# A short causal convolution moved from rows to columns in a two-block decoder on one core

## The chip, the core and the metric

The kernel runs on one core of one Trainium2 chip. It is one launch. The metric is the device time of the whole program in microseconds (us); less is better. The core has five engines with queues of their own: TensorE (PE in the profile, with its weight loads as PEld), VectorE (DVE), ScalarE (ACT), GpSimd (POOL) and SyncE (SP), which here issues all DMAs. Each queue is worked in order.

## What is computed

The program is two layers of a hybrid block and four layers of a second block, on a sequence of 256 rows of 1024 float32 values. The change touches one part of the two hybrid layers, a gated convolution over three neighbouring rows whose 256 columns are the first of the eight column blocks that the mixer's output projection takes:

```python
def short_conv_mixer(gate_b, gate_c, h, conv_w):
    u = gate_c * h
    u_pad = jnp.pad(u, ((0, 0), (CONV_K - 1, 0), (0, 0)))     # CONV_K = 3
    y = conv_w[0] * u_pad[:, 0:S]
    for j in range(1, CONV_K):
        y = y + conv_w[j] * u_pad[:, j:j + S]
    return gate_b * y
```

Row r of the result needs rows r, r-1 and r-2 of u. The result, transposed, is two of the eight 128-row blocks of yT, from which the output projection `mix` is computed; the other six come from two attentions.

## The kernel before

The 256 rows are two tiles of 128, t = 0 and t = 1. Each tile is worked by a generator ("thread") that runs through all layers; a driver at the end of the kernel gives both threads one weight block after another, thread 1 some blocks behind thread 0 (one block in the conv's projections F and H, two in the blocks mkv behind them). A weight block is loaded by one DMA on SP into one of five raw buffers, and split by ACT (the rounded high part, `wh`, L280) and DVE (the rest, `wl`, L233); each product is three matmuls (L322, `mm3`). `proj` (L380) asks for four weight blocks, does six matmuls with each and calls `flush` behind every block. `flush` also works off lists of deferred pieces: `due[t]` holds pairs of a count and a function, and each flush of thread t counts down and calls what has come to 0.

The program is then put in order by a scheduler in the framework, engine by engine, so the order in a queue isn't the order of the code. The tiles come from pools with a fixed number of buffers for each tag; a tile waits until the one that had its buffer has been read for the last time. PSUM banks with the tag `pj` are two for both threads together.

Around the conv, in `mixer` (L608 to L790): the projection F gives gate_b and gate_c, which ACT copies into `cf` (128 x 512, L756). The projection H gives h. DVE multiplies u = gate_c * h (L762). The shifted rows of u are wanted in the partitions of the rows that use them, so two DMAs per tile copy u into `up`, shifted by two rows and by one (L768), and for t = 1 two more bring the last rows of tile 0 (L770). Then DVE multiplies both shifted copies with tap rows `cw` that lie in all partitions (L773), adds (L774), POOL multiplies the third tap (L775), DVE adds it and multiplies with the gate (L776, L777), PE transposes the two halves against the identity (`transpose4`, L275, into `ycp`), and `cut` splits the result into yT's high part (ACT, L313) and low part (DVE, L314).

The projections `mkv` come next (`memory_block`): keys and values of the memory, from `memHi` and `memLo`. Layer 0 has three of these blocks there, layer 1 two. They don't use the conv's result; the output projection `mix` behind them does. The second attention of the layer (`six_heads`: `sp`, `ss`, `ptp`, `ET`) is interleaved with them. All conv instructions run four times: two layers, two tiles.

Of the kernel before, what the change touches and what calls it, by code (L numbers as in the profile page):

```python
# [8 lines left out]
F32 = mybir.dt.float32  # L9
# [3 lines left out]
ALU = mybir.AluOpType  # L13
AX = mybir.AxisListType

P = 128
D = 1024
ALPHA = 4.0 ** 0.25
IALPHA = 1.0 / ALPHA
# [17 lines left out]
EB = ("E", 2)  # L37
# [11 lines left out]
def kernel(  # L49
# [7 lines left out]
    nc = tc.nc  # L57
    V, S, G, T = nc.vector, nc.scalar, nc.gpsimd, nc.tensor

    const = ctx.enter_context(tc.tile_pool(name="const", bufs=1))  # L60
    wr = ctx.enter_context(tc.tile_pool(name="wr", bufs=RBUFS))
    wp = ctx.enter_context(tc.tile_pool(name="wp", bufs=WBUFS))
    sb = ctx.enter_context(tc.tile_pool(name="sb", bufs=1))
# [4 lines left out]
    tiles = {}  # L68
    shared = {}
# [4 lines left out]
    def colblock(key, mat, c0, n, gain=None):  # L74

        v = mat.rearrange("(k p) n -> p k n", p=P)
        for i in range(4):
            plan.append((key + (i,), "w", [P, 2, n], v[:, 2 * i:2 * i + 2, c0:c0 + n],
                         gain and (gain[0], gain[1], 2 * i)))

    def rowblock(key, mat, kts):
        v = mat.rearrange("(k p) n -> p k n", p=P)
        for i, k in enumerate(kts):
            plan.append((key + (i,), "w", [P, 1, D], v[:, k:k + 1, :], None))

    def aux(key, tag, shape, src):
        plan.append((key, tag, shape, src, None))

    def bcast_row(ap2d):
        n = ap2d.shape[-1]  # L90
        return ap2d.broadcast(0, P) if hasattr(ap2d, "broadcast") else ap2d.partition_broadcast(P)

    def memory_blocks(l, pos):
        return [j for j in range(4) if MKV[l, j] == pos]

    def fill(l, which):
        for m in range(2):
            for j in memory_blocks(m, (l, which)):
                colblock(("mkv", m, j), w_mkv[m], 512 * j, 512)
# [4 lines left out]
    for l in range(2):  # L104
        for nm, c0, n in MIXG:
            if nm == "cq" and l == 0:
                for t in range(2):
                    aux(("memr", t), "kv", [P, D], mem[t * P:(t + 1) * P, :])
            if nm == "cq":
                aux(("BT", l), "big8", [P, 6, 256], relx[l])  # L110
                aux(("cw", l), "grow", [P, 3, 256], bcast_row(conv_w[l:l + 1, :, :]))
            colblock((nm, l), w_in[l], c0, n)
        for j in memory_blocks(l, "M"):
            colblock(("mkv", l, j), w_mkv[l], 512 * j, 512)
        rowblock(("mix", l), w_mix[l], MIXK)
        for which in range(3):
            if which == 0:
                fill(l, 0)
            if which == 1:
                for j in range(2):  # L120
                    colblock(("mq", l, j), w_mq[l], 512 * j, 512)
            if l == 1 and which == 2:
                aux(("lnGB",), "big8", [P, 2, D], bcast_row(ln_rows[l, which:which + 1, :, :]))
            if which == 1:
                rowblock(("mo", l), w_mo[l], list(range(8)))
                fill(l, 1)
            if which == 2:
                for j in range(9):
                    if j < 8:
                        colblock(("ff1", l, j), w_ff1[l], 512 * j, 512)  # L130
                    if j > 0:
                        rowblock(("ff2", l, j - 1), w_ff2[l], list(range(4 * j - 4, 4 * j)))
                fill(l, 2)
    FG = [(512 * j, min(512, 2816 - 512 * j)) for j in range(6)]
    for i in range(4):
# [32 lines left out]
        for j in range(7):  # L168
            if j < 6:
                c0, n = FG[j]  # L170
                colblock(("fg", i, j), ffn_in[i], c0, n, (i, 1))
                colblock(("fu", i, j), ffn_in[i], 2816 + c0, n, (i, 1))
            if j > 0:
                c0, n = FG[j - 1]
# [7 lines left out]
    wnum, n = {}, 0  # L182
# [70 lines left out]
    lnc = const.tile([P, 2, 3, 2, 8], F32, name="lnc")  # L253
    ngc = const.tile([P, 4, 3, 8], F32, name="ngc")
    gbs = const.tile([P, 8], F32, name="gbs")

    def load_columns():
        nc.sync.dma_start(lnc, ln_cols)
        nc.sync.dma_start(ngc, ng_cols)
        nc.sync.dma_start(gbs, gm_bs)  # L260

# [10 lines left out]
    def transpose4(t, srcs, nm, kind="tr"):  # L272
        p = bank(kind, t, [P, 4, P], nm)
        for i, s in enumerate(srcs):
            T.transpose(p[:, i, :], s, ident)  # L275
        return p

    def copy(eng, o, i):
        if eng == "s":
            S.copy(o, i)  # L280
        else:
            V.tensor_copy(o, i)
# [23 lines left out]
    def cut(bank, sl, src, scale=1.0, rows=slice(0, P), hi_eng="s"):  # L306

        hi, lo = bank[0][rows, sl, :], bank[1][rows, sl, :]
        if scale == 1.0:
            copy(hi_eng, hi, src)  # L310
            V.tensor_tensor(out=lo, in0=src, in1=hi.bitcast(F32), op=ALU.subtract)
        else:
            S.activation(hi, src, AF.Copy, scale=scale)  # L313
            V.scalar_tensor_tensor(out=lo, in0=src, scalar=scale, in1=hi.bitcast(F32), op0=ALU.mult,  # L314
                                   op1=ALU.subtract)
# [10 lines left out]
    due = ([], [])  # L326
# [260 lines left out]
    def get2(key, shape, tag, bufs=1):  # L587

        if key not in shared:
            shared[key] = sb.tile(shape, F32, tag=tag, name="_".join(str(s) for s in key), bufs=bufs)  # L590
        return shared[key]
# [16 lines left out]
    def mixer(t, l, xT):  # L608
# [4 lines left out]
        yT = Parts()  # L613
# [15 lines left out]
        p = transpose4(t, [I[:, 0:128], I[:, 128:256], ik4.rearrange("p a d -> p (a d)")], "iqp")  # L629
# [10 lines left out]
        p = transpose4(t, [DQ[:, i * P:(i + 1) * P] for i in range(4)], "dqp")  # L640
# [6 lines left out]
        for b0 in (0, 2):  # L647
# [6 lines left out]
            for b in range(2):  # L654
                rv = sb.tile([P, 2, nk], F32, tag=EB[0].format(t=t), name="rl", bufs=EB[1])
                S.activation(rv, ips[b], AF.Relu)
                for i in range(2):
# [3 lines left out]
                    else:  # L661
                        V.scalar_tensor_tensor(out=score, in0=rv[:, i, :], scalar=iws[:, h:h + 1], in1=score,
                                               op0=ALU.mult, op1=ALU.add)
# [91 lines left out]
        cf = sb.tile([P, 512], F32, tag=f"rB{t}", name="cf", bufs=2)  # L755
# [2 lines left out]
                  lambda kt, h: shared[("cv", l, kt)][:, 64 * h:64 * h + 64],  # L758
                  lambda hs: BT[:, hs[0]:hs[-1] + 1:2, 256 - nk:256], lambda j: divmod(2 + j, 4)))
        pH = yield from proj(t, xT, ("H", l), 256)  # L760
        u = get2(("u", l, t), [P, 256], f"U{t}", 3)
        V.tensor_tensor(out=u, in0=cf[:, 256:512], in1=pH[:, 0:256], op=ALU.mult)  # L762

        up = sb.tile([P, 2, 256], F32, tag=EB[0].format(t=t), name="up", bufs=EB[1])
        if t == 0:
            G.memset(up[0:2], 0.0)
        for s_, d in enumerate((2, 1)):
            nc.sync.dma_start(up[d:P, s_, :], u[0:P - d, :])  # L768
            if t == 1:
                nc.sync.dma_start(up[0:d, s_, :], shared[("u", l, 0)][P - d:P, :])  # L770
        cw = tiles[("cw", l)]
        yc = sb.tile([P, 2, 256], F32, tag=f"rB{t}", name="yc", bufs=2)
        V.tensor_tensor(out=yc, in0=up, in1=cw[:, 0:2, :], op=ALU.mult)  # L773
        V.tensor_tensor(out=yc[:, 0, :], in0=yc[:, 0, :], in1=yc[:, 1, :], op=ALU.add)  # L774
        G.tensor_tensor(out=yc[:, 1, :], in0=u, in1=cw[:, 2, :], op=ALU.mult)  # L775
        V.tensor_tensor(out=yc[:, 0, :], in0=yc[:, 0, :], in1=yc[:, 1, :], op=ALU.add)  # L776
        V.tensor_tensor(out=yc[:, 0, :], in0=yc[:, 0, :], in1=cf[:, 0:256], op=ALU.mult)  # L777
        p = transpose4(t, [yc[:, 0, 0:P], yc[:, 0, P:2 * P]], "ycp")
        cut(yT.banks[0], slice(0, 2), p[:, 0:2, :], IALPHA)

        mems = memory_blocks(l, "M")
        for j in mems[:1]:
# [534 lines left out]
```

## Time and profile before

| what | value |
|---|---|
| device time, median of 3 runs | 2618.29 us (2616.46 to 2618.94) |
| device time of the profiled execution | 2621.53 us |
| span of its trace | 2619.8 us |
| PE busy (weight loads apart) | 2554.4 us, 98% |
| DVE busy | 1815.6 us, 69% |
| ACT busy | 1505.8 us, 57% |
| POOL busy | 62.9 us, 2% |
| DMA | 502.80 MB, mean 192 GB/s |

A row of the timeline gives the start (us from the span's start), the duration, the engine, the source line, the operation, the tile written and the tiles read with their shapes, and in brackets how long the engine had been idle before it and what ended that. Matmuls are pipelined: a row's duration is longer than the time to the next row's start. "PEclk" is the clock that TensorE was granted, as a share of full speed.

### The profile page before, as it was taken

What the parts mean: (1) busy time and instruction counts of PE and PEld (TensorE: products, weight loads), DVE (VectorE), ACT (ScalarE), POOL (GpSimd) and SP (SyncE); (2) the same over time, 40 slices, a digit from 0 to 9 for tenths busy, and PEclk for the clock granted to TensorE, in tenths of its full rate; (3) what the DMA queues carried; (4) which work ended last, traced back from release to release, by engine and by line L of the source; (5) the groups of instructions that cost most, each with busy time, mean ns of one, the idle gap of its engine ahead of it and who ended that gap; (6) DMA issues with size and microseconds to landing.
All of it is one profiled execution on the core that took longest, in us unless ns stands there. A gap on an engine that the chain in (4) does not pass through costs nothing. (4 is left out here: it accounts for less than half of the span.)

```text
span 2619.8 us, 36087 instructions
## 1 busy us (share of the span) xinstructions
PE 2554.4 (98%) x12300; PEld 2084.1 (80%) x12300; DVE 1815.6 (69%) x3321; ACT 1505.8 (57%) x2844; POOL 62.9 (2%) x92
## 2 busy tenths in 40 slices
PE   8899999989999999999999999999999999999998
PEld 7678787868788787788788888887787887877887
DVE  8665766866666776666766767667777667766666
ACT  5544555645455665555766666556656557655555
POOL 0000000000000000000000000000100000000000
PEclk9999999999999999999999999999999999999999
DMA  6453776445377666676755455766576775666764
GB/s 215 126 175 113 214 242 202 142 152 177 116 233 242 200 198 206 205 229 203 223 172 153 145 161 153 233 205 211 164 260 207 229 216 184 201 201 186 232 201 148
DMA packets 280736, 502.80 MB, mean 192 GB/s; under 512 B 27376, under 2 KB 101224, under 8 KB 279400
## 3 DMA queue, kind: packets, MB, share of 16 engines
q1 hardware_dynamic: 280552, 500.50, 62.0%
q8 instruction: 96, 1.57, 0.3%
q14 instruction: 88, 0.72, 0.1%
HBM read 472.11 MB, written 27.26 MB: 191 GB/s over the span
## 5 line engine op out<-in xcount | busy, mean ns | idle before, releaser
L322 PE MATMUL pj<-wh,part 128*128 128x512 f32 (+3 forms) x4480 | 1426.3, 385 | 1.5 <-ACT part L280 1.3
L322 PEld LDWEIGHTS pj<-wh,part 128*128 128x128 f32 x4480 | 832.3, 189 | 166.9 <-issue 9.1
L322 PE MATMUL pj<-wl,part 128*128 128x512 f32 (+3 forms) x2240 | 852.8, 381 | 1.6 <-DVE wl L229 1.3
L322 PE MATMUL acc<-wh,part 128*128 128x512 f32 x1920 | 581.5, 395 | 13.8 <-ACT part L280 7.3
L322 PEld LDWEIGHTS pj<-wl,part 128*128 128x128 f32 x2240 | 422.6, 189 | 77.3 <-issue 3.1
L322 PEld LDWEIGHTS acc<-wh,part 128*128 128x128 f32 x1920 | 357.3, 189 | 93.6 <-ACT part L280 9.7
L322 PE MATMUL acc<-wl,part 128*128 128x512 f32 x960 | 308.0, 394 | 0.2
L233 DVE TENSOR_TENSOR wl<-ff,wh 128x512 fp32r<-128x512 f32 x256 | 170.2, 686 | 106.9 <-ACT wh L280 106.8
L280 ACT CAST wh<-ff 128x512 fp32r<-128x512 f32 x256 | 152.9, 620 | 139.2 <-PE acc L322 68.4
L322 PEld LDWEIGHTS acc<-wl,part 128*128 128x128 f32 x960 | 181.0, 189 | 38.8 <-DVE wl L233 0.8
L226 ACT ACTIVATE wh<-fg,ngc 128x512 fp32r<-128x512 f32 (+1 forms) x192 | 126.8, 686 | 121.3 <-PE pj L322 63.9
L229 DVE SCALAR_TENSOR_TENSOR wl<-fg,ngc,wh 128x512 fp32r<-128x512 f32 (+1 forms) x192 | 129.5, 702 | 80.9 <-ACT wh L226 80.9
L229 DVE SCALAR_TENSOR_TENSOR wl<-fu,ngc,wh 128x512 fp32r<-128x512 f32 (+1 forms) x192 | 128.2, 704 | 51.8 <-ACT wh L226 48.4
L226 ACT ACTIVATE wh<-fu,ngc 128x512 fp32r<-128x512 f32 (+1 forms) x192 | 123.8, 684 | 59.9 <-PE acc L322 35.4
L280 ACT CAST wh<-fo 128x512 fp32r<-128x512 f32 x176 | 103.5, 621 | 78.1 <-PE pj L322 76.4
L233 DVE TENSOR_TENSOR wl<-fo,wh 128x512 fp32r<-128x512 f32 x176 | 115.0, 684 | 44.7 <-ACT wh L280 39.0
L226 ACT ACTIVATE wh<-rv,ngc 128x512 fp32r<-128x512 f32 x64 | 45.2, 722 | 40.9 <-PE pj L322 33.6
L229 DVE SCALAR_TENSOR_TENSOR wl<-rv,ngc,wh 128x512 fp32r<-128x512 f32 x64 | 46.7, 747 | 24.5 <-ACT wh L226 24.3
L233 DVE TENSOR_TENSOR wl<-ro,wh 128x512 fp32r<-128x512 f32 x64 | 43.3, 688 | 27.8 <-ACT wh L280 26.5
L233 DVE TENSOR_TENSOR wl<-mkv,wh 128x512 fp32r<-128x512 f32 x64 | 42.5, 688 | 27.4 <-ACT wh L280 27.3
L229 DVE SCALAR_TENSOR_TENSOR wl<-pg,ngc,wh 128x512 fp32r<-128x512 f32 x64 | 46.6, 748 | 21.4 <-ACT wh L226 20.6
L280 ACT CAST wh<-mkv 128x512 fp32r<-128x512 f32 x64 | 37.1, 618 | 39.8 <-PE acc L322 19.4
(323 smaller groups left out, 3230.5 us busy)
## 6 DMA issues: line engine op xcount, KB each, us to landing
ff<-in_w_ff_dram SPq DMA_DIRECT2D x128, 512.0 KB, 4.3
fo<-in_ffn_out_dram SPq DMA_DIRECT2D x88, 512.0 KB, 4.3
fg<-in_ffn_in_dram SPq DMA_DIRECT2D x80, 512.0 KB, 4.4
fu<-in_ffn_in_dram SPq DMA_DIRECT2D x80, 512.0 KB, 4.2
xd<-xt SPq DMA_DIRECT2D x384, 64.0 KB, 2.3
mkv<-in_w_mkv_dram SPq DMA_DIRECT2D x32, 512.0 KB, 4.8
rv<-in_ret_in_dram SPq DMA_DIRECT2D x32, 512.0 KB, 4.5
rg<-in_ret_in_dram SPq DMA_DIRECT2D x32, 512.0 KB, 4.1
```

The lines of the kernel that those rows point to most:

```text
L226: S.activation(h_, r_, AF.Copy, scale=gc)
L229: V.scalar_tensor_tensor(out=l_, in0=r_, scalar=gc, in1=h_.bitcast(F32), op0=ALU.mult, op1=ALU.subtract)
L233: (V if le == "v" else G).tensor_tensor(out=l_, in0=r_, in1=h_.bitcast(F32), op=ALU.subtract)
L280: S.copy(o, i)
L322: T.matmul(outs[i], a, ws[i][b], start=s0, stop=s1)
```

## The change

Both factors of the conv are transposed first, and the conv is done on the transposed values: there a row is a column, a shift by one row is a shift by one element within a partition, and a tap is one scalar per partition.

DVE multiplies u into the second half of `cf` (after's L765). `turn_conv`, put on `due` with a count of 1, lets PE transpose all four 128-column pieces of `cf` (two of the gate, two of u) into one PSUM bank; ACT copies u's half into `ut`, which is as long as the sequence plus two zero columns (L776), and the gate's half into `gt` (L777). `ut` and `gt` are parts of one tile `cu` for both threads, in the buffer `grow` that the tap rows had. `taps`, with a count of 2, is DVE's: for each of two column blocks one multiplication with the first tap (L782) and two multiply-adds with the others (L784), then the gate (L786), and `cut` into yT, now from SBUF. The `up` copies, the tiles `u`, `up` and `yc`, POOL's multiplication and the two loads of `cw` (384 KB each) are gone. The taps as columns, `cwc`, come by four DMAs of 128 partitions x 3 single words in `load_columns`, which is called once near the start. Here is the diff:

```diff
@@ the plan of loads @@
                 aux(("BT", l), "big8", [P, 6, 256], relx[l])
-                aux(("cw", l), "grow", [P, 3, 256], bcast_row(conv_w[l:l + 1, :, :]))
@@ constants @@
+    cwc = const.tile([P, 2, 2, 3], F32, name="cwc")
 
     def load_columns():
         nc.sync.dma_start(lnc, ln_cols)
+        with nc.allow_non_contiguous_dma(reason="a few words a partition"):
+            for l in range(2):
+                for c in range(2):
+                    nc.sync.dma_start(cwc[:, l, c, :], conv_w[l, :, c * P:(c + 1) * P].rearrange("j p -> p j"))
         nc.sync.dma_start(ngc, ng_cols)
         nc.sync.dma_start(gbs, gm_bs)
@@ mixer @@
         pH = yield from proj(t, xT, ("H", l), 256)
-        u = get2(("u", l, t), [P, 256], f"U{t}", 3)
-        V.tensor_tensor(out=u, in0=cf[:, 256:512], in1=pH[:, 0:256], op=ALU.mult)
-
-        up = sb.tile([P, 2, 256], F32, tag=EB[0].format(t=t), name="up", bufs=EB[1])
-        if t == 0:
-            G.memset(up[0:2], 0.0)
-        for s_, d in enumerate((2, 1)):
-            nc.sync.dma_start(up[d:P, s_, :], u[0:P - d, :])
-            if t == 1:
-                nc.sync.dma_start(up[0:d, s_, :], shared[("u", l, 0)][P - d:P, :])
-        cw = tiles[("cw", l)]
-        yc = sb.tile([P, 2, 256], F32, tag=f"rB{t}", name="yc", bufs=2)
-        V.tensor_tensor(out=yc, in0=up, in1=cw[:, 0:2, :], op=ALU.mult)
-        V.tensor_tensor(out=yc[:, 0, :], in0=yc[:, 0, :], in1=yc[:, 1, :], op=ALU.add)
-        G.tensor_tensor(out=yc[:, 1, :], in0=u, in1=cw[:, 2, :], op=ALU.mult)
-        V.tensor_tensor(out=yc[:, 0, :], in0=yc[:, 0, :], in1=yc[:, 1, :], op=ALU.add)
-        V.tensor_tensor(out=yc[:, 0, :], in0=yc[:, 0, :], in1=cf[:, 0:256], op=ALU.mult)
-        p = transpose4(t, [yc[:, 0, 0:P], yc[:, 0, P:2 * P]], "ycp")
-        cut(yT.banks[0], slice(0, 2), p[:, 0:2, :], IALPHA)
+        V.tensor_tensor(out=cf[:, 256:512], in0=cf[:, 256:512], in1=pH[:, 0:256], op=ALU.mult)
+
+        cu = get2(("cu", l), [P, 772], "grow", 1)
+        ut = cu[:, 0:516].rearrange("p (c n) -> p c n", c=2)
+        gt = cu[:, 516:772].rearrange("p (c n) -> p c n", c=2)
+        o = P * t
+
+        def turn_conv():
+            p = transpose4(t, [cf[:, i * P:(i + 1) * P] for i in range(4)], "ycp")
+            if t == 0:
+                G.memset(ut[:, :, 0:2], 0.0)
+            S.copy(ut[:, :, o + 2:o + P + 2], p[:, 2:4, :])
+            S.copy(gt, p[:, 0:2, :])
+
+        def taps():
+            y = cf[:, 0:256].rearrange("p (c n) -> p c n", c=2)
+            for c in range(2):
+                V.tensor_scalar(out=y[:, c, :], in0=ut[:, c, o:o + P], scalar1=cwc[:, l, c, 0:1], scalar2=None, op0=ALU.mult)
+                for j in (1, 2):
+                    V.scalar_tensor_tensor(out=y[:, c, :], in0=ut[:, c, o + j:o + P + j], scalar=cwc[:, l, c, j:j + 1],
+                                           in1=y[:, c, :], op0=ALU.mult, op1=ALU.add)
+            V.tensor_tensor(out=y, in0=y, in1=gt, op=ALU.mult)
+            cut(yT.banks[0], slice(0, 2), y, IALPHA)
+
+        due[t].append([1, turn_conv])
+        due[t].append([2, taps])
+        due[t].sort(key=lambda d: d[0])
```

The scheduler makes another order of this. In layer 0, tile names carry buffer numbers, of which only the groups matter here: `pj_1358` (before) and `pj_1346` (after) are tile 0's first mkv bank, `pj_1455` and `pj_1443` tile 1's; `cf_1148` and `cf_1213` are tile 0's and tile 1's cf. A bracket names the engines whose semaphore the instruction waits for.

On PE in layer 0 before, at the end of tile 0's first mkv block, a row's transposes `ycp` stand behind a wait for DVE, and tile 1's second mkv weight block is queued behind them:

```order
L322 MATMUL pj_1358<-wl_1463,memHi0_691 128x512
L275 MATMUL ptp_1478<-tab_75,ss_1419 128x128 [waits DVE_49,PE_49]
L275 MATMUL ptp_1478<-tab_75,ss_1419 128x128
L322 MATMUL pj_1358<-wh_1462,memLo_102 128x512
L275 MATMUL ycp_1353<-tab_75,yc_1347 128x128 [waits DVE_49]
L275 MATMUL ycp_1353<-tab_75,yc_1347 128x128
L322 MATMUL pj_1455<-wh_1379,memHi1_743 128x512
```

On PE in layer 0 now, one weight block further forward, u's two transposes of tile 0 (the gate's two stand 19 rows earlier) come in the middle of the first mkv block:

```order
L326 MATMUL pj_1346<-wl_1335,memHi0_694 128x512
L326 MATMUL pj_1346<-wh_1334,memLo_103 128x512
L279 MATMUL ycp_1381<-tab_75,cf_1148 128x128 x2
L326 MATMUL pj_1346<-wh_1367,memHi0_694 128x512
L717 MATMUL ptp_1321<-ET_1326,cv_0_0_1002 64x128 [waits Activation_49]
```

The transposes have moved ahead of four weight blocks (tile 0's second, third and fourth and tile 1's first), and what they read is the product u and no longer the finished conv.

On DVE in layer 0 before, behind the copy `ET` of tile 1's attention, tile 1's u comes at once, and tile 0's wait for the DMAs into `up` five rows later:

```order
L282 COPY ET_1316<-ptp_1311 128x512 [waits PE_49]
L762 TENSOR_TENSOR u_0_1_1437<-cf_1210,pj_1212 128x256
L233 TENSOR_TENSOR wl_1459<-mkv_0_0_3_1213,wh_1458 128x512 [waits DMAHW4_49]
L233 TENSOR_TENSOR wl_1463<-mkv_0_0_3_1213,wh_1462 128x512
L314 SCALAR_TENSOR_TENSOR part1_215<-ptp_1311,part1_214 64x256 [waits Activation_49]
L314 SCALAR_TENSOR_TENSOR part1_215<-ptp_1318,part1_214 64x256 [waits Activation_49]
L233 TENSOR_TENSOR wl_1491<-mkv_0_1_0_1275,wh_1490 128x512 [waits DMAHW5_49]
L773 TENSOR_TENSOR yc_1347<-up_1343,cw_0_247 128x512 [waits DMAHW2_49,DMAHW0_49,Pool_49]
```

On DVE in layer 0 now, from the middle of tile 0's taps to the product u of tile 1 (the copy `ET`, the two `wl` of mkv_0_0_3 and the two L782 of tile 0 stand just ahead of the first row, and the L782 wait for ACT):

```order
L318 SCALAR_TENSOR_TENSOR part1_216<-ptp_1314,part1_215 64x256 [waits Activation_49]
L318 SCALAR_TENSOR_TENSOR part1_216<-ptp_1321,part1_215 64x256 [waits Activation_49]
L784 SCALAR_TENSOR_TENSOR cf_1148<-cu_0_1345,cwc_94,cf_1148 128x128 [waits DVE_49] x4
L689 SCALAR_TENSOR_TENSOR ss_1424<-sp_1420,BT_0_246 128x256 [waits PE_49]
L786 TENSOR_TENSOR cf_1148<-cf_1148,cu_0_1345 128x256 [waits DVE_49]
L692 TENSOR_REDUCE nmx1_1426<-ss_1424 128x1 [waits DVE_49]
L689 SCALAR_TENSOR_TENSOR ss_1433<-sp_1421,BT_0_246 128x256 [waits PE_49]
L318 SCALAR_TENSOR_TENSOR part0_123<-cf_1148,part0_122 128x256 [waits Activation_49]
L698 RECIPROCAL rcs1_1430<-sume1_1428 128x1 [waits Activation_49]
L692 TENSOR_REDUCE nmx1_1435<-ss_1433 128x1 [waits DVE_49]
L700 TENSOR_SCALAR ss_1424<-ss_1424,rcs1_1430 128x256 [waits DVE_49]
L765 TENSOR_TENSOR cf_1213<-cf_1213,pj_1215 128x256
```

Tile 1's u has moved from behind `ET` to behind the whole of tile 0's taps.

The third place is on PE, where tile 1's first mkv bank takes over the bank that tile 1's projection H had. Before, its rows wait for nothing:

```order
L322 MATMUL pj_1358<-wl_1400,memHi0_691 128x512
L322 MATMUL pj_1358<-wh_1399,memLo_102 128x512
L322 MATMUL pj_1455<-wh_1327,memHi1_743 128x512
L322 MATMUL pj_1455<-wl_1328,memHi1_743 128x512
L322 MATMUL pj_1455<-wh_1327,memLo_102 128x512
```

Now they wait for DVE, which must have read H's bank in L765 (`pj_1215`), and two transposes of tile 1's attention, which wait for L700 above, stand three rows ahead:

```order
L279 MATMUL ptp_1473<-tab_75,ss_1424 128x128 [waits DVE_49,PE_49]
L279 MATMUL ptp_1473<-tab_75,ss_1424 128x128
L326 MATMUL pj_1346<-wh_1450,memLo_103 128x512
L326 MATMUL pj_1443<-wh_1330,memHi1_746 128x512 [waits DVE_49]
L326 MATMUL pj_1443<-wl_1331,memHi1_746 128x512
```

Tile 1's first mkv weight block stood ahead of tile 0's fourth before, and stands behind it now.

## The prediction

> **What bounds the kernel now.** I read the page's busy times first, then PE's waits, then the timeline at the conv, then the stages' granted clock.
>
> ```profile
> span 2619.8 us, 36087 instructions
> PE 2554.4 (98%) x12300; PEld 2084.1 (80%) x12300; DVE 1815.6 (69%) x3321; ACT 1505.8 (57%) x2844; POOL 62.9 (2%) x92
> PE ycp L275 <- DVE yc L777: 13.1, 3, 5.2
> PE ptp L275 <- DVE ss L696: 7.1, 8, 5.2
> ```
>
> PE is busy for 98% of the span, so the program ends earlier only if PE works less, waits less or runs at a better clock. All its idle time is 2619.8 - 2554.4 = 65.4 us. The list of PE's waits (us in total, times, longest) begins with the conv: 13.1 us in three waits for the finished conv `yc`. The fourth hides under another name, the 5.2 us wait of `ptp` for `ss`. The timeline shows what DVE and PE do at the four convs, DVE's row first and PE's behind it:
>
> ```profile
> 113.96 0.69 DVE L773 TENSOR_TENSOR yc<-up,cw 128x512 f32<-128x512 f32 x1 [5.19 <-DMA up<-u]
> 117.98 0.66 PE L275 MATMUL ptp<-tab,ss 128*128 128x128 f32 x2 [5.15 <-DVE ss L696]
> ...
> 128.87 0.69 DVE L773 TENSOR_TENSOR yc<-up,cw 128x512 f32<-128x512 f32 x1 [3.67 <-DMA up<-u]
> 133.14 0.44 PE L275 MATMUL ycp<-tab,yc 128*128 128x128 f32 x2 [3.71 <-DVE yc L777]
> ...
> 560.47 0.69 DVE L773 TENSOR_TENSOR yc<-up,cw 128x512 f32<-128x512 f32 x1 [5.28 <-DMA up<-u]
> 564.04 0.69 PE L275 MATMUL ycp<-tab,yc 128*128 128x128 f32 x2 [5.24 <-DVE yc L777]
> ...
> 575.65 0.69 DVE L773 TENSOR_TENSOR yc<-up,cw 128x512 f32<-128x512 f32 x1 [4.39 <-DMA up<-u]
> 579.92 0.44 PE L275 MATMUL ycp<-tab,yc 128*128 128x128 f32 x2 [4.17 <-DVE yc L777]
> ```
>
> DVE stands still until the shifted copies of u have landed, and behind L773 in its queue stand the attention's `ss` and the weight splits. So the attention's softmax is late as well, and PE's wait for `ss` at 117.98 is the same stall. PE's four: 5.15 + 3.71 + 5.24 + 4.17 = 18.27 us, more than a quarter of all its idle time.
>
> The waits cost more than their length. The six microseconds behind each, and six undisturbed ones for comparison (the columns are length, busy time of PE, PEld, DVE, ACT, POOL, then PE's granted clock, DMA share, GB/s):
>
> ```profile
> 117.98:123.98 6.00, 6.00 (x23) 4.30 (x24) 3.79 (x10) 2.79 (x8) 0.00 (x0) 0.55 0.43 150
> 133.14:139.14 6.00, 6.00 (x25) 4.98 (x26) 4.38 (x8) 2.62 (x5) 0.00 (x0) 0.72 0.65 208
> 564.04:570.04 6.00, 6.00 (x27) 4.66 (x28) 4.96 (x13) 3.45 (x9) 0.00 (x0) 0.74 0.56 190
> 579.92:585.92 6.00, 6.00 (x25) 4.86 (x26) 4.69 (x8) 2.61 (x5) 0.00 (x0) 0.72 0.70 221
> ...
> 140.00:146.00 6.00, 6.00 (x30) 4.96 (x29) 3.48 (x6) 3.08 (x5) 0.00 (x0) 1.00 0.73 249
> ```
>
> After each wait PE has work but a lower clock. What is lost is (1 - clock) times 6 us: 2.70 + 1.68 + 1.56 + 1.68 = 7.62 us. Stalls and slow clock together: 18.27 + 7.62 = 25.9 us.
>
> **Part by part.** *The stall goes.* No DMA lies between u and the conv's result any more, so all 25.9 us are open to the change. What is late next is DVE's own chain in the third order piece above; I follow it for layer 0 with these rows of before:
>
> ```profile
> 104.81 0.69 DVE L282 COPY ET<-ptp 128x512 f32<-128x512 f32 x1
> 105.35 1.14 ACT L280 CAST wh<-mkv 128x512 fp32r<-128x512 f32 x2
> 105.87 1.28 DVE L233 TENSOR_TENSOR wl<-mkv,wh 128x512 fp32r<-128x512 f32 x2
> 106.93 0.50 PE L322 MATMUL pj<-wh,memLo 128*128 128x512 f32 x1
> 107.17 0.88 DVE L314 SCALAR_TENSOR_TENSOR part<-ptp,part 64x256 fp32r<-64x256 f32 x2
> ...
> 26.93 0.38 ACT L631 COPY iqT<-iqp 128x256 f32<-128x256 f32 x1 [1.65 <-PE iqp L275]
> 31.46 0.28 DVE L660 TENSOR_SCALAR score<-rl,iws 128x128 f32<-128x128 f32 x1
> 34.42 1.19 DVE L662 SCALAR_TENSOR_TENSOR score<-rl,iws,score 128x128 f32<-128x128 f32 x3
> 115.36 0.41 DVE L688 TENSOR_REDUCE nmx<-ss 128x1 f32<-128x256 f32 x1
> 115.69 0.41 DVE L685 SCALAR_TENSOR_TENSOR ss<-sp,BT 128x256 f32<-128x256 f32 x1
> ```
>
> ACT's two copies of tile 0 (0.38 each, like the copy at 26.93) follow the first cast of 105.35, so they end near 106.7. DVE has done `ET` and two `wl` by about 106.8 (u of tile 1 is no longer between them). Then: two L782 at 0.28, to 107.4; two L318 at 0.44, to 108.3; four L784 in a chain at 1.19 / 3 = 0.40, to 109.9; five operations of 256 columns at 0.33 apart (115.36 to 115.69), to 111.5; reciprocal, reduction and L700, to about 112.6; L765 to 113.0. PE comes from 106.93 through sixteen matmuls of 512 columns at 0.24 (142.29 to 142.53 below), 3.8 us, and some 1.3 us of two half as long, four `sp` and two transposes (an estimate at half that spacing and a little for the turns), and reaches `ptp_1473` near 112.0. It waits 0.6 us for L700; L765, which frees the bank for `pj_1443`, comes 0.4 us behind and is there as PE gets to it. Tile 1's own taps have no transposes behind them, and `mix` comes blocks later. So I charge 0.7 us in each layer, **1.4 us**. The new waits stand in that chain: L782 for ACT's copies, with L318 and `ss` queued behind it, which PE's `sp` and `ptp` want; ACT's L776 for PE's transposes, which read a product that stands well ahead in DVE's queue; and L777 of tile 1 for tile 0's L786, long done. From below: nothing, if DVE runs 0.7 us ahead of my count. From above: 4 us in each layer, about the waits of before (3.71 to 5.24).
>
> *PE's added work* is eight 128 x 128 transposes, two for each conv. Four like them in a stream of matmuls:
>
> ```profile
> 142.29 0.39 PE L322 MATMUL pj<-wh,memLo 128*128 128x512 f32 x1
> 142.53 0.60 PE L275 MATMUL mkp<-tab,mk 128*128 128x128 f32 x4
> 142.88 0.48 PE L322 MATMUL pj<-wh,memHi 128*128 128x512 f32 x1
> 143.20 0.39 PE L322 MATMUL pj<-wl,memHi 128*128 128x512 f32 x1
> ```
>
> From 142.53 to 142.88 are 0.35 us, and the matmul behind them takes 0.32 to the next in place of 0.24: 0.43 for four, 0.11 for one, **0.9 us** for eight. The Trainium skill's TensorE: Matmul & The Clock Gate (Part 4: PE-mode transpose) gives about 275 ns for one in a kernel (bf16), which would be 2.2 us here, an estimate; these rows say otherwise, and the sum goes by them.
>
> *DVE and ACT.* For one conv DVE loses u, L773 (0.69), L774, L776, L777 and the last cut (0.4 each), 2.7 us; it gains L765, two L782, four L784, L786 and the cut, 0.4 + 0.56 + 1.6 + 0.8 = 3.4. ACT gains two copies, 0.8. Over the stage,
>
> ```profile
> 100.00:150.00 50.00, 40.91 (x198) 31.94 (x198) 30.06 (x63) 21.94 (x49) 2.28 (x3) 0.90 0.49 161
> ```
>
> DVE does 30.06 us in 50. With 1.4 more and the stage 12 us shorter that is 31.5 in 38, 83%: covered by PE's stream, but with little left for bunching; if it isn't, it shows in the wait above. POOL's L775 and SP's twelve copies cost nothing where they go away: SP waits for free buffers there.
>
> *The loads near the start.* `cwc` adds 4 x 384 = 1536 words of 4 bytes in SP's queue ahead of `cq_3`, and `cw` (384 KB) goes from ahead of `cq_0`.
>
> ```profile
> 4.12 0.48 SPq L252 DMA_DIRECT2D pos_i<-in_positions_dram  x1
> 8.00:9.00 1.00, 0.00 (x0) 0.00 (x1) 0.77 (x2) 0.74 (x2) 0.00 (x0) 1.00 1.07 356
> ...
> 23.56 0.38 SPq L200 DMA_DIRECT2D cq<-in_w_in_dram  x1
> 30.00:32.00 2.00, 2.00 (x12) 1.59 (x13) 2.00 (x9) 2.00 (x7) 0.00 (x0) 1.00 0.03 9
> 34.44 0.51 ACT L280 CAST wh<-cq 128x384 fp32r<-128x384 f32 x1
> ```
>
> SP takes 0.5 us for an issue of single words (`pos_i`, 256 of them), so `cq_3` is issued near 25.1 in place of 23.56, and the 1.5 us are covered: its data is cast at 34.44, and the DMA engines are empty at 30 to 32. While words like `pos_i`'s ran among the weights, 356 GB/s still moved. Value taken: **0**. The scheduler also reorders the DVE work of the first 60 us, between a gain of 1 us (little PE idle time is there to win) and a loss of 2 us, by the size of the waits that reordering can move, like the 0.9 us of PE's wait `mTp`:
>
> ```profile
> 53.66 0.66 PE L275 MATMUL mTp<-tab,memr 128*128 128x128 f32 x4 [0.92 <-ACT cqT L732]
> ```
>
> *The sum*: -25.9 + 1.4 + 0.9 + 0 = **-23.6 us**. From the profiled execution, 2621.53 us (its span and 1.7 us around it), that gives 2597.9. This execution lies 3.2 us above the median of the three runs, 2618.29, so the forecast in their terms is 2618.3 - 23.6 = **2595 us**.
>
> **Rivals.** *DVE gives a part back.* The taps, the softmax and the splits bunch, and PE waits 3 to 6 us in each layer in place of 0.7. For it: DVE at 83%, and L765 at the end of a long row. Against it: where no DMA is in the chain, PE's waits for DVE are short: seven of the eight waits of `ptp` for `ss` come to 7.1 - 5.2 = 1.9 us. Time: 2595 - 1.4 + 6 to 12, 2600 to 2605.
>
> *The column loads hold the early weights up.* If each copy of single words were a round trip on its own, `cq_3` and `ck_0` would land late and ACT, which casts in order, would stand. The nearest row for such a trip is the whole 512 KB load's 4.3 us to landing:
>
> ```profile
> ff<-in_w_ff_dram SPq DMA_DIRECT2D x128, 512.0 KB, 4.3
> ```
>
> Four in a row are 17.2 us. Between the issue of `cq_3` and its cast lie 10.9 us, of which 4.3 are its own way, so it would be 17.2 - 6.6 = 10.6 us late: 2606 us if none of that is covered. Against it: the copies are issued without waiting for each other. The Trainium skill speaks against the change here: DMA: Bandwidth & Descriptors (Rules for kernel authors) says a strided last dimension becomes one descriptor per element and should be rearranged to be contiguous. The trace shows no loss at the 256 words of `pos_i`; 1536 no row shows.
>
> *The gain is spent elsewhere*: PE arrives earlier at the `mix` weights and waits for them, with all but 5 us of it gone, 2613 to 2618. Against it: in the stage the DMA engines are at 0.49.
>
> *Slower.* One mechanism: `pj_1443` can't start before L765, which stands behind tile 0's taps, which wait for ACT's copies, which stand behind casts that wait for a load. One late load then stops three engines, in both layers, at that place. With a wait w and 1.7 us of slow clock behind it the change is at -25.9 + 0.9 + 2 x (w + 1.7), slower than before from w = 10.8 us on; at w = 14 it gives 2624.7 us. ACT's longest wait for a load here is 7.04 us, and it stood behind the `up` copies on SP:
>
> ```profile
> 576.67 1.86 ACT L280 CAST wh<-mix 128x512 fp32r<-128x512 f32 x3 [7.04 <-DMA mix<-in_w_mix_dram]
> ```
>
> **The numbers.** Forecast 0.75, DVE gives back 0.12, late column loads 0.06, spent elsewhere 0.04, slower 0.03. A measurement of this kernel tells about 0.2% (5.2 us) from no change; the first three are faster by more, 0.93; no change 0.04; slower 0.03. The range: at its low end no wait in the stage and a gain of 1 us at the start, with 1 to 2 us for a slow clock that I read too small, 2595 - 1.4 - 1 - 2 = 2590; at its high end 2604, the upper bound of the waits (8 in place of 1.4) with 2 us at the start, which takes in most of the DVE case; the last three cases, 0.13, and its tail stay out.
>
> **What would show it.** Right: no PE wait over 1 us between 100 and 150 and none in the same stage of layer 1, PEclk 1.00 there, and tile 1's `mkv` rows some 13 us earlier. The DVE rival shows as waits of `ptp` or `pj` for L700 or L765, the early-load rival as ACT waiting for `cq` or `ck`. The forecast is wrong if PE's idle time falls by less than 13 us, or if the clock falls below 1.00 in places where it was full.

## The result and the profile after

The changed kernel takes 2597.24 us (median of 4 runs, 2594.81 to 2599.94) against 2618.61 us (4 runs, 2616.46 to 2620.57): 21.4 us less, ratio 0.9915 with a 95% interval of 0.9903 to 0.9928, which is 19 to 25 us. A second measurement, beside the first three experiments, gave 2593.56 against 2618.82: 25.3 us less, ratio 0.9910 (0.9896 to 0.9923). Forecast were 2595 us and 23.6 us less.

The page's head of after, and the parts of its list of PE's waits (us in total, times, longest) that matter here:

```profile
span 2593.1 us, 36098 instructions
PE 2546.9 (98%) x12308; PEld 2079.4 (80%) x12308; DVE 1815.5 (70%) x3333; ACT 1509.7 (58%) x2852; POOL 58.6 (2%) x88
...
PE acc L326 <- ACT part L284: 6.3, 5, 2.5
PE xTp L279 <- DMA row<-in_x_dram: 6.0, 2, 4.4
...
PE ptp L279 <- DVE ss L700: 2.4, 5, 1.3
```

The waits of `ycp` are gone from the list, and those of `ptp` have fallen from 7.1 us to 2.4. PE's idle time is 2593.1 - 2546.9 = 46.2 us in place of 65.4, 19.2 less. PE's busy time is 7.5 us shorter, though it does eight matmuls more: the slow clock is gone from the two stages. The stage of layer 0 (100 to 150) and that of layer 1 (540 to 590), here layer 1 of before, then both of after (the columns as in the prediction):

```profile
540.00:590.00 50.00, 40.18 (x217) 31.10 (x217) 31.81 (x73) 23.32 (x61) 2.28 (x3) 0.93 0.44 141
```

```profile
100.00:150.00 50.00, 49.87 (x269) 40.76 (x269) 35.69 (x78) 28.98 (x61) 0.11 (x1) 1.00 0.59 186
540.00:590.00 50.00, 49.67 (x249) 40.63 (x247) 33.47 (x71) 24.31 (x48) 0.86 (x1) 1.00 0.62 204
```

PE is busy for 49.9 and 49.7 us of 50, where it was busy for 40.9 and 40.2, and its clock is 1.00 in both. Where in the program the time was won shows in rows that both kernels have. The first is an attention step ahead of the first conv, the others the transposes of the memory's keys (`mkp`) in and behind the stages; of before:

```profile
98.18 1.03 PE L713 MATMUL ptp<-ET,cv 128*64 128x128 f32 x11
...
461.74 0.60 PE L275 MATMUL mkp<-tab,mk 128*128 128x128 f32 x4
...
583.90 0.76 PE L275 MATMUL mkp<-tab,mk 128*128 128x128 f32 x4
```

and of after:

```profile
97.10 1.14 PE L717 MATMUL ptp<-ET,cv 128*64 128x128 f32 x12
...
128.48 0.60 PE L279 MATMUL mkp<-tab,mk 128*128 128x128 f32 x4
...
446.45 0.60 PE L279 MATMUL mkp<-tab,mk 128*128 128x128 f32 x4
...
556.11 0.60 PE L279 MATMUL mkp<-tab,mk 128*128 128x128 f32 x4
```

After is 1.1 us ahead before the first conv, 14.1 us behind it (142.53 was before's row), 15.3 us ahead of layer 1's stage, 27.8 us behind it, and 26.7 us at the end. The two stages give 13.0 and 12.5 us, 25.5 in all. Between them the lead grows by 1.2 us, and behind them it drifts between 25 and 28 us.

These two executions differ by 26.7 us and the medians by 21.4, because each execution loses some clock elsewhere too. For each trace I summed (1 - PEclk) x 4 us over all stretches of 4 us in which PE works, for instance

```profile
116.00:120.00 4.00, 2.02 (x7) 1.77 (x8) 3.43 (x11) 2.87 (x8) 0.30 (x1) 0.57 0.57 197
120.00:124.00 4.00, 4.00 (x17) 2.58 (x17) 2.36 (x5) 1.92 (x5) 0.00 (x0) 0.57 0.26 68
```

of before, and parted the sum into the conv stages and the rest of the program (a stretch that is partly idle is counted whole, so the first column is a little high where PE waits):

| trace | span | clock lost in the conv stages | elsewhere |
|---|---|---|---|
| before | 2619.8 | 8.5 | 3.4 |
| after | 2593.1 | 0 | 5.2 |
| after, second measurement | 2590.1 | 0 | 1.7 |
| no copies (below) | 2597.7 | 0 | 10.3 |
| 126 + 1 rows (below) | 2593.8 | 0 | 5.1 |
| 112 + 15 rows (below) | 2593.3 | 0 | 3.4 |
| columns four times (below) | 2595.5 | 0 | 6.8 |

Elsewhere 1.7 to 10.3 us are lost, with no pattern by kernel in these single executions. Taken off the span, the six traces without the wait all come to 2587.4 to 2589.9 us. The 2.5 us that are left between them no run explains; the wait for the input rows at the start, 6.0 to 6.9 us in these six, is at most 0.9 of it.

### The profile page after: what moved, and what is told of

Same layout as the page of the kernel before. It is cut to its first block, busy times and chain, and to the rows that moved or that the text cites. A ratio compares the mean times of both kernels' runs of the same rounds, so it can differ in the third digit from the quotient of the medians.

```text
span 2593.1 us, 36098 instructions
## 1 busy us (share of the span) xinstructions
PE 2546.9 (98%) x12308; PEld 2079.4 (80%) x12308; DVE 1815.5 (70%) x3333; ACT 1509.7 (58%) x2852; POOL 58.6 (2%) x88
## 2 busy tenths in 40 slices
DMA packets 280904, 500.97 MB, mean 193 GB/s; under 512 B 28816, under 2 KB 101648, under 8 KB 279568
## 5 line engine op out<-in xcount | busy, mean ns | idle before, releaser
L225 ACT ACTIVATE wh<-rv,ngc 128x512 fp32r<-128x512 f32 x64 | 45.2, 722 | 40.9 <-PE pj L326 33.6
L232 DVE TENSOR_TENSOR wl<-mkv,wh 128x512 fp32r<-128x512 f32 x64 | 41.9, 686 | 26.7 <-ACT wh L284 26.5
L284 ACT CAST wh<-ro 128x512 fp32r<-128x512 f32 x64 | 39.3, 620 | 36.1 <-PE pj L326 28.6
```

The source lines that it names most:

```text
L225: S.activation(h_, r_, AF.Copy, scale=gc)
L232: (V if le == "v" else G).tensor_tensor(out=l_, in0=r_, in1=h_.bitcast(F32), op=ALU.subtract)
```

## The experiments

My theory on record is that the waits for the shifted copies and the slow clock behind them are the whole gain. The rivals are that the layout itself pays, that the copies cost by what they hold up, and the prediction's three on DVE, the column loads and the later stages. Each experiment stands against before on the same chip.

### The copies left out

```diff
-        up = sb.tile([P, 2, 256], F32, tag=EB[0].format(t=t), name="up", bufs=EB[1])
...
-            nc.sync.dma_start(up[d:P, s_, :], u[0:P - d, :])
-            if t == 1:
-                nc.sync.dma_start(up[0:d, s_, :], shared[("u", l, 0)][P - d:P, :])
...
-        V.tensor_tensor(out=yc, in0=up, in1=cw[:, 0:2, :], op=ALU.mult)
+        V.tensor_tensor(out=yc, in0=u.rearrange("p (o k) -> p o k", o=1).to_broadcast([P, 2, 256]), in1=cw[:, 0:2, :],
+                        op=ALU.mult)
```

> Before, with the copies into up left out: the product with the first two tap rows reads u itself, so the shift by rows is left out of the result; all else stays (two transposes for a conv, POOL's product, tap rows). My theory is that the four waits for the copies, 18.3 us, and the slow clock behind them, 7.6 us, are the whole of what the change gains: 25.9 us less, 2590 to 2595 us against 2618.6, PE waits of under 1 us at the four convs and PEclk 1.00 behind them. Rival: the column layout itself pays (DVE's queue in another order); then the rows without copies give less than half, over 2606 us.

Measured: 2594.02 us against 2618.82, ratio 0.9909 (0.9895 to 0.9923), 24.8 us less. The stage of layer 0 has 48.76 us of PE in 50 at a clock of 1.00. The old layout without the copies is as fast as the new one, so the layout itself isn't what pays.

### The copy of 127 rows cut in two

```diff
-            nc.sync.dma_start(up[d:P, s_, :], u[0:P - d, :])
+            nc.sync.dma_start(up[d:d + 126, s_, :], u[0:126, :])
+            if d == 1:
+                nc.sync.dma_start(up[127:P, s_, :], u[126:127, :])
```

> Before, with the copy of 127 rows (the shift by one) cut into one of 126 rows and one of a single row; nothing is left out. The shift by two has 126 rows already. In the trace of before the DMA engines are at 0.06 to 0.07 of 16, which is one engine, and move 24 GB/s from 112 to 114, until the copies have landed; 127 rows of 1 KB at 24 GB/s are 5.4 us. Theory A: it is this one copy on one engine that DVE waits for; with 126 rows on many engines the copies land about 5 us earlier, and of the waits of 5.2, 3.7, 5.2 and 4.2 us under 1 us each is left: 2591 to 2598 us. Theory B: it is the fixed way of a DMA between two SBUF tiles and the weights ahead of it in the engines' queues; then the waits stay over 3 us each and the time over 2611.

Measured: 2594.95 us against 2618.82, ratio 0.9910 (0.9896 to 0.9923), 23.9 us less, with all of before's layout, transposes and DMAs. Before, in 112 to 114, just ahead of the landing that DVE waits for:

```profile
112.00:113.00 1.00, 0.83 (x4) 0.37 (x2) 0.00 (x0) 0.00 (x0) 0.00 (x0) 1.00 0.07 24
113.00:114.00 1.00, 0.00 (x0) 0.00 (x0) 0.04 (x1) 0.00 (x0) 0.00 (x0) 1.00 0.06 24
```

With 126 + 1 rows, the time from issue to landing of `up`'s copies, as far as the trace has it (copies of one row), DVE's first product with `up` of tile 0, and the stage of layer 0:

```profile
DMA to landing us min/median/max: 1.7/1.8/2.1
```

```profile
106.16 0.69 DVE L775 TENSOR_TENSOR yc<-up,cw 128x512 f32<-128x512 f32 x1 [0.34 <-DMA up<-u]
```

```profile
100.00:150.00 50.00, 49.53 (x253) 39.48 (x253) 35.77 (x71) 26.08 (x56) 2.29 (x3) 1.00 0.59 203
```

In before about one of 16 DMA engines is at work (0.07 and 0.06 of 16 are 1.1 and 1.0) and 24 GB/s move; the copy of 127 rows of 1 KB needs 5.4 us so. The trace has no landing time for the copies of 126 rows, but DVE's product starts 2.6 us after the issue of tile 0's last copy began (103.56), with a wait of 0.34 us in place of 5.19; in layer 1 the wait is 0.32 us, and for tile 1 there is none. Theory A holds: DVE waited for one copy that lay on one engine. The rate of that copy can be read for tile 0 only: while tile 1's runs in before, weights fill the engines (348 GB/s from 126 to 127). But its wait goes with the same cut.

### 113 + 14 rows, and 112 + 15

The diff is that of 113 + 14; the other kernel has 112 and 113 in the places of 113 and 114.

```diff
+            m = 113 if d == 1 else 126
-            nc.sync.dma_start(up[d:P, s_, :], u[0:P - d, :])
+            nc.sync.dma_start(up[d:d + m, s_, :], u[0:m, :])
+            if d == 1:
+                nc.sync.dma_start(up[114:P, s_, :], u[113:127, :])
```

> As the kernel with 126 + 1 rows, which took 2595 us, but the copy of 127 rows is cut into 113 + 14: as many DMAs, and fewer rows in the larger. Theory: the rows go to as many engines as divide their number, up to 16; 113 is prime as 127 is, so one engine moves 113 KB, 4.8 us at 24 GB/s, and the waits come back 0.6 us shorter than before: 2612 to 2617 us. Rival: any cut helps, since 127 rows are merely too many for one step, or since the last row alone is what goes slowly; then it is like 126 + 1: 2593 to 2598 us.

> As the kernel with 113 + 14 rows, which took 2620.5 us beside 2617.5 of before, but cut into 112 + 15: one row is in the other piece, nothing else differs. Theory (a copy goes to as many engines as divide its number of rows, up to 16): 112 goes to 16 engines and 15 to 15, no copy lies on one engine, the waits go: 2591 to 2598 us. Rival (the last row alone, or pieces of more than about 15 rows in a second copy, make the difference): the waits stay, 2612 to 2621 us.

Measured: 113 + 14 takes 2620.54 us against 2617.49, ratio 1.0015 (1.0005 to 1.0024), and 112 + 15 takes 2596.06 against 2620.91, ratio 0.9906 (0.9884 to 0.9928). One row in the other piece is worth some 28 us. PE's waits with 113 + 14:

```profile
PE sp L680 <- DVE part L314: 9.8, 2, 4.9
PE ycp L275 <- DVE yc L780: 7.7, 2, 4.4
```

and the landings with 112 + 15 (of the copies of 112, 15 and 1 rows; those of 126 have none in the trace):

```profile
DMA to landing us min/median/max: 1.6/2.0/2.5
```

113 + 14 has 17.5 us of waits, 0.8 less than before, where I had expected 2.4 less, but 3.5 us more of slow clock in the stages (12.0 in place of 8.5, by the sum over stretches of 4 us), which is why it is no faster: the clock is at 0.50 for the whole six microseconds behind the two waits of 4.9 us.

```profile
113.12:119.12 6.00, 6.00 (x12) 3.68 (x13) 4.06 (x9) 0.86 (x2) 0.73 (x1) 0.50 0.23 72
561.49:567.49 6.00, 6.00 (x13) 3.67 (x14) 4.05 (x9) 0.63 (x2) 0.72 (x1) 0.50 0.25 89
```

So it isn't the size of the copy that counts, but the number of its rows as a number. The Trainium skill says so in DMA: Bandwidth & Descriptors (Why a DMA increments its semaphore by 16 and not by 1): a copy is spread over the largest number of engines up to 16 that divides the size of the slowest dimension on both of its sides, and 127 partitions go to one. These traces agree in the cases that they show: 127 and 113, both prime, at 24 GB/s or with the waits, 126 + 1 and 112 + 15 without.

### The slow copy kept, and hidden

```diff
-        up = sb.tile([P, 2, 256], F32, tag=EB[0].format(t=t), name="up", bufs=EB[1])
+        up = sb.tile([P, 2, 256], F32, tag=f"rA{t}", name="up", bufs=2)
...
+        def conv():
+            V.tensor_tensor(out=up, in0=up, in1=cw[:, 0:2, :], op=ALU.mult)
...
+            cut(yT.banks[0], slice(0, 2), p[:, 0:2, :], IALPHA)
+
+        due[t].append([5, conv])
+        due[t].sort(key=lambda d: d[0])
```

> Before, with the copies as they were (127 rows, one engine) and issued where they were, but everything behind them put on due with a count of 5, and up in a buffer that is free there; nothing is left out. In the order, layer 0's transposes of the conv stand 18 matmuls later for tile 0 and 13 later for tile 1, 4.3 and 3.1 us at 0.24. Theory: only the wait costs, not the slow copy; of the waits of 5.2, 3.7, 5.2 and 4.2 us about 1 us each is left, and with little clock lost behind them 2593 to 2602 us. Rival: the slow copies hold the mkv weights up on SP and in the DMA engines; then PE waits for casts of mkv instead, and the time stays over 2606 us.

A first form, with a buffer of its own for `up`, needed more SBUF than there was (a pool of 5 KB per partition, 1.06 KB left) and has no time.

Measured: 2605.98 us against 2617.49, ratio 0.9965 (0.9950 to 0.9981): 11.5 us less, half of the change's gain. My expectation failed and the rival's mechanism came true, though the time is 0.02 us short of its 2606. In layer 0 SP, ACT, DVE and PE, in this order:

```profile
107.34 5.53 SPq L200 DMA_DIRECT2D mkv<-in_w_mkv_dram  x1
119.94 1.14 ACT L280 CAST wh<-mkv 128x512 fp32r<-128x512 f32 x2 [5.50 <-DMA mkv<-in_w_mkv_dram]
121.28 0.61 DVE L314 SCALAR_TENSOR_TENSOR part<-ptp,part 64x128 fp32r<-64x128 f32 x2 [5.80 <-ACT part L313]
122.45 0.66 PE L275 MATMUL ycp<-tab,up 128*128 128x128 f32 x2 [5.28 <-issue]
```

No one waits for `up` any more. But SP, which issues a weight load in 0.37 us elsewhere, is held for 5.53 us at the load behind the copies, and meanwhile the engines move next to nothing:

```profile
110.00:112.00 2.00, 2.00 (x12) 1.62 (x10) 2.00 (x8) 0.38 (x2) 0.00 (x0) 1.00 0.07 25
```

The weights come late, ACT's cast waits 5.50 us, DVE and PE behind it. Layer 1 has the same at 561 (PE waits 5.77 us, SP is held for 5.50). Together 11.1 us of waits and 5.2 us of slow clock (0.63 and 0.50 over the six microseconds behind them) are left of 25.9. Copies on one engine can thus cost twice: whoever reads them waits, and the loads behind them come late. The order differs from before's here, though: both tiles' six copies stand together on SP (101.47 to 107.23), where before issues tile 1's 15 us behind tile 0's and holds SP for 1.11 us at most.

### PE given useless work during the wait

```diff
+        p = bank("tr", t, [P, 4, P], "ycp")
+        for i in range(40):
+            T.transpose(p[:, 2, :], up[:, 0, 0:P], ident)
```

> Before, with 40 more transposes of the first shifted copy (126 rows, which lands early) ahead of each conv's own two; what they write is overwritten. They give PE 4.4 us of work (40 x 0.11) of no use while the 127 rows are under way, so PE's idle time there falls and the time at which the conv is ready does not. Theory: the lower clock behind the four waits (7.6 us) comes from PE standing still; with the fill it stays at 1.00 and the time falls by 5 to 8 us, to 2611 to 2614 us, though PE has 17.6 us more to do. Rival: the clock falls for another reason at that place; then the time is unchanged or longer, 2617 to 2624 us, and PEclk in the six microseconds behind is 0.55 to 0.75 as before.

Measured: 2643.8 us against 2617.49, ratio 1.0107 (1.0092 to 1.0122), 26.3 us more. It doesn't tell the two apart, because the fill isn't in the wait. PE's and DVE's rows in layer 0:

```profile
105.67 4.59 PE L780 MATMUL ycp<-tab,up 128*128 128x128 f32 x40
...
118.08 1.22 PE L680 MATMUL sp<-ckT,cqT 64*128 64x256 f32 x2 [5.66 <-DVE part L314]
```

```profile
113.40 0.69 DVE L773 TENSOR_TENSOR yc<-up,cw 128x512 f32<-128x512 f32 x1 [5.59 <-DMA up<-u]
```

The scheduler put the 40 transposes ahead, but in turn moved the attention's `sp` behind rows of DVE that stand behind L773, so PE ran dry at the same time with less done. The four waits are 19.6 us, no shorter than before, and behind each the clock is low again. That the clock stays up if PE is kept busy wasn't shown in this way.

### The new chain loaded: longer taps, more transposes, more column loads

```diff
             V.tensor_tensor(out=y, in0=y, in1=gt, op=ALU.mult)
+            for _ in range(6):
+                for c in range(2):
+                    V.tensor_scalar(out=y[:, c, :], in0=y[:, c, :], scalar1=1.0, scalar2=None, op0=ALU.mult)
```

> The changed kernel with twelve more multiplications by 1.0 on 128 x 128 for each conv, between the gate product L786 and the cut; nothing is left out. At the 0.20 us at which the two L782 follow each other that is 2.4 us of DVE for a conv, and tile 0's stand ahead of L700 and L765 of tile 1. Theory A (DVE has no slack left in this stage, it is busy for 22.5 of the 24 us from 100 to 124): PE's wait of 0.2 us for L700 grows to some 2.6 us in each layer, with some slow clock behind it, 2600 to 2605 us. Theory B (PE's stream covers DVE): under 1 us each, 2594 to 2598 us.

Measured: 2597.50 us against 2617.49, ratio 0.9927 (0.9913 to 0.9942): 20.0 us less, against 21.4 and 25.3 for the changed kernel. The stage's first 24 us in after and with the longer taps:

```profile
100.00:124.00 24.00, 23.87 (x136) 18.78 (x136) 22.52 (x58) 16.39 (x40) 0.11 (x1) 1.00 0.54 168
```

```profile
100.00:124.00 24.00, 23.50 (x133) 18.24 (x132) 22.54 (x77) 14.81 (x40) 0.39 (x1) 1.00 0.40 123
```

```profile
PE pj L326 <- ACT mk L813: 0.5, 1, 0.5
PE ptp L279 <- DVE ss L700: 0.4, 1, 0.4
```

DVE was at 94% of these 24 us already. The added work pushes other work of DVE's out of the stretch, and PE loses 0.4 us more in it. By the rows that both traces have (97.10, 128.48, 446.45 and 556.11 in after; 97.32, 130.48, 449.52 and 560.17 here), the stage of layer 0 costs 1.8 us more and that of layer 1 1.0. The time is theory B's; the 1.8 us lie between B's "under 1 us" and A's 2.6, so PE's stream covers most of the added work, with little left over.

```diff
+            for _ in range(4):
+                for i in range(4):
+                    T.transpose(p[:, i, :], cf[:, i * P:(i + 1) * P], ident)
```

> The changed kernel with each conv's four transposes done five times into the same bank: 64 transposes more in all. At the 0.11 us each that the prediction read from rows of before that is 7.0 us more than the changed kernel, 2601 to 2604 us. At the 275 ns of the Trainium skill (TensorE: Matmul & The Clock Gate, Part 4) it is 17.6 us more, 2611 to 2615 us.

Measured: 2608.16 us against 2621.71, ratio 0.9944 (0.9929 to 0.9958), 13.6 us less, so 7.8 to 11.7 us slower than the changed kernel by its two measurements. Fourteen of the added ones in a row, and the next matmul:

```profile
109.88 1.75 PE L776 MATMUL ycp<-tab,cf 128*128 128x128 f32 x14
111.38 0.48 PE L326 MATMUL pj<-wh,memHi 128*128 128x512 f32 x1
```

14 in 1.50 us are 0.107 us each, 6.9 us for 64. The rest of the difference isn't shown to be theirs: this trace has a wait of 1.9 us and a slow clock at 64 to 76 us, ahead of the first conv. What keeps the other three runs as slow (2604.88 to 2608.41 us) stays open.

```diff
-            for l in range(2):
+            for l in [0, 1] * 4:
```

> The changed kernel with the four loads of the tap columns done four times: twelve DMAs of 384 single words more, ahead of the weights cq_3 and ck_0 on SP. In the trace of the changed kernel the four take 2.68 us of SP's time, so twelve take 8.0 us. Theory A: only SP's issue time counts, and most of it is covered: cq_3 is issued at 34 in place of 25.9, PE's idle time in the first 60 us grows by 2 to 7 us, 2597 to 2603 us. Theory B: each is a round trip of its own, 5.9 us to landing in the trace, before the next starts: 12 x 5.9 = 71 us late, of which at least 50 show: over 2640 us. Theory C: single words cost nothing at all: no change, under 1 us.

Measured: 2597.07 us against 2621.71, ratio 0.9904 (0.9887 to 0.9920), 24.6 us less, as the change itself. The first 60 us of before, of after and with sixteen loads:

```profile
0.00:60.00 60.00, 51.45 (x289) 45.74 (x291) 47.74 (x177) 34.80 (x78) 0.59 (x7) 1.00 0.64 204
```

```profile
0.00:60.00 60.00, 51.73 (x296) 45.63 (x297) 49.86 (x180) 35.91 (x80) 0.62 (x8) 1.00 0.67 209
```

```profile
0.00:60.00 60.00, 51.59 (x292) 45.87 (x293) 48.52 (x177) 34.95 (x78) 0.62 (x8) 1.00 0.69 202
```

PE is idle for 8.55, 8.27 and 8.41 us. The last casts of `cq` do come 5.7 us later with sixteen loads (39.57 in place of 33.86), and nothing shows of it in the time. Theory A's cover is wider than I thought, and C describes the time; B, the prediction's rival, falls.

## Why the prediction was right, and where not

- *The stall, -18.3.* Right. PE's idle time fell by 19.2 us, of which 1.1 is a shorter wait for the input rows at the very start, in which the kernels don't differ (7.1 and 6.0; other traces have 6.2 to 6.9, with the second wait of these transposes counted where the list names another releaser for it).
- *The slow clock, -7.6.* Right: PE's busy time fell by 7.5 us with 0.9 us of work added, the two stages gave 25.5 us, which leaves 7.2 beside the 18.3 of waits, 8.1 with the added 0.9 put back, and all eight traces without the long waits have a clock of 1.00 in both stages. Waits alone would have given 17 us. That idleness causes the drop is inferred from where it comes; the attempt to fill the wait failed.
- *DVE's chain as the next wait, +1.4.* Too high: PE doesn't wait there. All its idle time from 100 to 150 is 0.13 us, at 104, ahead of this chain, and from 540 to 580 it has none. The place is where the longer taps later made a wait of 0.4 us, but the prices were too high. DVE's rows of after there:

```profile
106.83 1.14 DVE L784 SCALAR_TENSOR_TENSOR cf<-cu,cwc,cf 128x128 f32<-128x128 f32 x4
...
110.22 0.34 DVE L700 TENSOR_SCALAR ss<-ss,rcs 128x256 f32<-128x256 f32 x1
110.48 0.41 DVE L765 TENSOR_TENSOR cf<-cf,pj 128x256 f32<-128x256 f32 x1
```

and PE's first transposes behind L700:

```profile
110.78 0.38 PE L279 MATMUL ptp<-tab,ss 128*128 128x128 f32 x2
```

  The four L784 end 1.17 us after they began (the next row starts at 108.00): 0.29 each in place of 0.40. The three of L662, from which I had the price, take longer than these four (1.19 us and 1.14). PE comes to `ptp_1473` 4.8 us behind the matmul of `memLo` that starts the count (106.01 in after), where I had 5.1, and L765 ends 4.9 us behind it, where I had 6.1. L700 ends at 110.56, 0.22 us ahead of PE.
- *DVE's load.* 83% was forecast for 38 us; from 100 to 138 it is 31.14 us, 82%. It bunches: 94% in the first 24. The cover held, and the longer taps show how little is left.
- *The transposes, +0.9.* Right, 0.107 us each in the run with five times as many. The 275 ns that the Trainium skill gives in TensorE: Matmul & The Clock Gate (Part 4: PE-mode transpose) are near the duration of one row here, 272 ns in the median for `mkp`. But the next row starts 0.107 us later, and the sum needs that spacing.
- *The column loads, 0.* Right, and still 0 with four times as many. The Trainium skill's rule on strided last dimensions (DMA: Bandwidth & Descriptors, Rules for kernel authors) is no bar for 1536 words here. Its descriptor per element shows, though: twelve more loads of 384 words add 4800 packets under 512 B (33616 and 28816).
- *SP's twelve copies "cost nothing where they go away".* Wrong as an argument. SP did wait for free buffers in before, but with the wait for `up` hidden the slow copy costs some 11 us of waits through the weights behind it. In before the late weights lay beside the wait (ACT waited 5.9 us for `mkv` in 100 to 150, and not at all in after), so the sum didn't suffer.
- *The rivals.* DVE giving back: no, PE has no wait for it in the stages' convs. Gain spent elsewhere: no, 27.8 us ahead behind layer 1 and 26.7 at the end. Slower, through a late load and three engines: it didn't come; ACT's longest wait for a load in the stages is 1.3 us now (for `mix`), since the copies ahead of it are gone. I made no load late on purpose, so its price wasn't tried.
- *The signs.* No PE wait over 1 us is left in the stages, PEclk is 1.00 there, and tile 1's rows come 14 us earlier. One sign of being wrong came as well: the clock of after is 0.66 from 852 to 856, where before has 1.00 (its rows stand at 876 to 884). The second measurement has 1.00 there, so this goes with the execution and not with the change.
- *The sum*, -23.6, lies between the two measurements, -21.4 and -25.3. With nothing for DVE's chain it would be -25.0, beside the 25.5 that the two stages gave in the traces.

One thing the prediction took for granted: that a DMA between u and the conv must cost a wait. It was this DMA. The new layout removes the stall, but is not needed for it: two more lines in before's loop do the same within what can be measured (23.9 and 24.9 us less). No run was faster than the changed kernel by more than its two measurements differ.

## What to carry to other kernels

When a wait for a small DMA is long, look at the DMA engines' share and bandwidth in its last microseconds: one sixteenth at 24 GB/s points to a number of rows without a divisor from 2 to 16, and a cut into pieces that have one (126 + 1, 112 + 15, not 113 + 14) costs one more issue. Try that before a redesign, and don't count on hiding such a copy, since the loads behind it can come late too. Price a PE wait of over 3 us with the slow clock behind it, here 7.6 us on top of 18.3.

## What the runs showed of the hardware

- A copy of 127 KB in 127 rows moved at 24 GB/s. As 112 + 15 rows both pieces landed in 2.2 us in the median, and as 126 + 1 rows DVE had them 2.6 us after the last issue began. While slow copies were under way, SP's issue of one load took 5.53 us in place of 0.37. Why SP is held, rather than only the data, no run shows.
- The clock fell behind all 14 PE waits of 3.3 to 5.9 us (in before, 113 + 14, hidden copy and fill), and behind 5 of the 15 waits of 2.0 to 3.0 us that these and eight other traces have past the first 40 us. An example of after, with the stretch behind the wait, and one of its second measurement, where the clock stayed up:

```profile
850.82 0.82 PE L326 MATMUL acc<-wh,part 128*128 128x512 f32 x2 [2.52 <-ACT part L284]
```

```profile
852.00:856.00 4.00, 4.00 (x14) 3.17 (x13) 3.45 (x6) 2.11 (x4) 0.51 (x1) 0.66 0.27 103
```

```profile
852.00:856.00 4.00, 3.24 (x14) 2.69 (x15) 2.97 (x7) 2.41 (x5) 0.55 (x1) 1.00 0.45 146
```

  That the same place drops in one execution and not in another accounts for the 3 us between the two traces of the changed kernel (5.2 and 1.7 us lost outside the stages). The Trainium skill's TensorE: Matmul & The Clock Gate (Part 1: The HAM clock gate) has a free-running window of about 3.4 us of idleness behind the drop. That fits the chance in the short waits only in part: a drop behind a wait of 3.31 us, of 2.5 us, or, in after at 1776 (0.57 for 4 us), behind waits of 0.79 and 1.05 us is not what a window idle throughout would give. How idle a window must be no run shows.
